# Layer 1's sums of down weights by DMA from DRAM to DRAM during attention, and pairs 2 and 3 of its gate and up by Strassen's scheme

## The chip, the cores and the metric

The kernel runs on one core of a Trainium2 chip. The metric is the device time of one execution in microseconds; the time of a kernel is the median of its runs. Engine names as in the profile: PE is TensorE, PEld its weight loads, DVE is VectorE, ACT is ScalarE, POOL is GpSimd, SP is SyncE, which here only issues DMA.

## The reference

Two decoder layers over x of 512 tokens by 1024 columns. Layer 0 mixes tokens by causal pooling, layer 1 by differential attention with eight heads; behind each mixer stands a gated feed-forward net with 2816 hidden columns, and behind each of the four parts a LayerNorm.

```python
def _swiglu(x, w_gate, w_up, w_down):
    return (jax.nn.silu(x @ w_gate) * (x @ w_up)) @ w_down

def reference(x, pool_w, pool_scale, w_qkv, w_o, lam_p, subln_g, rel_table, w_gate,
              w_up, w_down, ln_mix_g, ln_mix_b, ln_ffn_g, ln_ffn_b):
    for i in range(DEPTH):
        j = i // N_MIXERS
        if i % N_MIXERS == 0:
            h = _multiscale_pool(x, pool_w[j], pool_scale[j])
        else:
            lambda_init = 0.8 - 0.6 * math.exp(-0.3 * i)
            h = _diff_attention(x, w_qkv[j], w_o[j], lam_p[j], subln_g[j], rel_table, lambda_init)
        x = _layernorm(ALPHA * x + h, ln_mix_g[i], ln_mix_b[i])
        x = _layernorm(ALPHA * x + _swiglu(x, w_gate[i], w_up[i], w_down[i]), ln_ffn_g[i], ln_ffn_b[i])
    return x
```

## The kernel before

**Numbers in two halves.** A float32 operand is held as two fp32r tiles: a high half, cast by ScalarE (`h`), and a low half, the operand minus the high half, written by VectorE (`l`). A product is three matmuls: high with high, high with low, low with high (`mm3`, lines 123 to 127, and line 806). All weights lie in one DRAM tensor, `wall`, in pieces of 128 x 1024 in the order of use. SyncE loads them into `raw` (five buffers, line 97), ScalarE and VectorE halve them into weight pairs (six buffers), TensorE multiplies.

**Gate and up.** The function `ffn(layer, late)` (line 449) runs the hidden columns in 11 pairs of 128-column blocks, k and k + 11. A *plain* pair has four chunks of weights, gate and up for both blocks, each against all of x (`plain`, line 758); a chunk is 8 x 3 matmuls of 512 columns. A *Strassen* pair (`strassen`, line 778) has seven products, named P1, Q5, P6, Q3, P7, P2, Q4, each 24 matmuls of 256 columns, into three banks A, C and B. Three products read quarters of x as they are. Four read sums of quarters of x, kept in the tile `xs` as blocks 0 to 3 (for Q5, P6, P7, Q3), each with its high and low half. Four of the seven weights are sums of the pair's four pieces: VectorE adds them in `raw` (line 552) before they are halved. The tuple `SPLIT` (line 47) says which pairs are Strassen pairs: 4 to 10, in both layers.

**The sums of x** are made by the generator `sums_of_x` (line 592), one step at each `next`: four half sums (line 597), four differences and sums of these (lines 612 to 621), with a cast to the high half by ScalarE (line 600) and a low half by VectorE (line 603) for each of the four blocks. The loops call it twice at the start (pair 0) and then twice for every `plain(f)` from f = 3 on (line 765), where f counts blocks, two to a pair.

**The first pairs.** The tokens' last quarters come late, so the first blocks (`early`: three in layer 0, two in layer 1) are run in two halves of the tokens (line 739); f = 2 and 3 are pair 1, f = 4 and 5 pair 2. With each block goes VectorE's product of Silu and up into `hid` (line 584), and with the first four blocks the scale and shift of the last LayerNorm (`affine`, lines 203 and 204, "res" in the profile). After each pair, `sum_hidden` (line 677) makes sums of hidden columns for the down products: four VectorE instructions of 256 columns, a cast, a low half and a store to `ssum`.

**Down.** The product of the hidden columns with the down weights is Strassen's scheme again: P1, Q5, P6, Q3, P7, P2, Q4 over six row groups (`PAIRS`). Four of the seven weight operands are sums of blocks of down weights. They are made during gate and up: for each of 11 rows `load_terms` (line 638) issues three DMAs on GpSimd's queue (two loads, line 651, and one that accumulates, line 652) into free rows of `hid` or the buffer of the LayerNorm parameters; `sum_terms` (line 655) does two VectorE additions of 512 columns (lines 657, 658) and two stores on ScalarE's queue (line 662) to the DRAM tile `tsum`. `weight_sums` (line 671) starts one row, at blocks 0, 1, 3, 5, 7 and at every Strassen pair but the last. The down products load their operands from `wall` and `tsum` (lines 486 and 489).

**Attention.** For every head, TensorE makes values, query and key, transposes the probabilities of the head before, mixes its values and scores the new head. GpSimd has one instruction per head there: the low half of the squares of a head's output (`sql`, line 108, called at 1123), which the sum over squares (`root`, line 1126) of the next head's turn needs.

**What sets the order.** The program runs under a manual schedule: on each engine and each DMA queue, instructions run in the order in which the code emits them; the framework adds only the waits. GpSimd's DMAs stand in GpSimd's own order.

Of the kernel before, what the change touches and what calls it, by code (L numbers as in the profile page):

```python
# [12 lines left out]
F32 = mybir.dt.float32  # L13
# [3 lines left out]
ALU = mybir.AluOpType  # L17

P = 128
# [6 lines left out]
FB = FF // P  # L26
# [17 lines left out]
RAWS = 5  # L44
HALF = FB // 2
DOWN = ("P1", "Q5", "P6", "Q3", "P7", "P2", "Q4")
SPLIT = (4, 5, 6, 7, 8, 9, 10)
GATE = ("P1", "Q5", "P6", "Q3", "P7", "P2", "Q4")
PAIRS = [(0, 2), (2, 2), (4, 2), (6, 2), (8, 2), (10, 1)]

# [2 lines left out]
def trunk(ctx, tc, x, wall, pscale, lam_p, subln, table, lng, lnb, band, first, onehot, out):  # L53
# [386 lines left out]

# [3 lines left out]
    def ffn(layer, late):  # L449
# [5 lines left out]
        with tc.tile_pool(name=f"ffn{layer}", bufs=1) as fp:  # L455
# [6 lines left out]


            order = [k + j * HALF for k in range(HALF) for j in range(2)]
            tsum = dram.tile([4, len(PAIRS), P, 1024], F32, name=f"tsum{layer}")
            ssum = dram.tile([P, 2, 2, HALF, 256], F32, name=f"ssum{layer}")

            def block(i, b):

                if PAIRS[i][1] == 2:  # L470
                    return wall[c1 + 4 * i + b]
                return wall[c1 + 20 + b // 2][:, (b % 2) * 512 : (b % 2 + 1) * 512]


            items = [(p, i) for p in DOWN for i in range(len(PAIRS))]
# [4 lines left out]
            def fetch_item(j):  # L480
                p, i = items[j]
                w = 512 * PAIRS[i][1]
                t = keep.tile([P, 1024], F32, tag="raw", name=f"r{layer}_{j}", bufs=RAWS)[:, :w]
                src = {"P1": 0, "P2": 2, "Q3": 3}
                if p in src:
                    nc.sync.dma_start(out=t, in_=block(i, src[p]))
                else:
                    m = {"Q5": 0, "P6": 3, "P7": 1, "Q4": 2}[p]
                    nc.sync.dma_start(out=t, in_=tsum[m, i, :, :w])
                drops[j] = t  # L490

            def refill():
# [21 lines left out]
            for k in range(HALF):  # L514
                j0 = index[k] = len(chunks)
                c = c0 + 4 * k
                if k in SPLIT:

                    chunks += [(c, ()), (c, (c, c + 1)), (c, (c, c + 2)), (c + 2, ())]
                    chunks += [(c + 1, (c + 1, c + 2)), (c + 3, ()), (c, (c, c + 3))]  # L520
                    step("cast", j0)
                    for w in (
                        "low 0, sum 1, cast 1, sum 4, cast 3, cast 4, low 1, sum 2, cast 2, low 3, "
                        "low 2, sum 6, cast 5, cast 6, low 4, low 5, low 6"
                    ).split(", "):
                        steps.append((w[:-2], j0 + int(w[-1])))
                else:
                    for i in range(4):
                        chunks.append((c + i, ()))
                        step("cast", j0 + i)  # L530
                        step("low", j0 + i)
# [33 lines left out]
            def ahead(upto):  # L565
                advance(upto)
                if upto > len(chunks):
                    prepare(upto - len(chunks), upto - len(chunks))
# [100 lines left out]
            behind = []  # L669

            def weight_sums():
                g = sum_terms(summed_rows[0])
                summed_rows[0] += 1
                next(g)
                behind.append(g)
# [18 lines left out]
            def catch_up():  # L694
                for g in list(behind):
                    if next(g, g) is g:
                        behind.remove(g)
# [35 lines left out]

            early = 3 if layer == 0 else 2
            accs = [(bank(f"g{layer}_{f}"), bank(f"u{layer}_{f}")) for f in range(early)]
            load_terms(0)
            load_terms(1)
            sums = sums_of_x()
            for lo in (0, 256):
                for f in range(early):  # L740
                    for i in range(2):
                        product(accs[f][i], 2 * f + i, lo, lo + 256)
                        if not lo and (f, i) in late:
                            late[f, i]()
                        if not lo:
                            advance(2 * early, True)
                    if lo:
                        advance(2 * f + 6)
                        gated(order[f], *accs[f])
                        affine(n - 1, f)  # L750
                        catch_up()
                        if f < 2:
                            weight_sums()
                            next(sums)
                        if f == 1:
                            behind.append(sum_hidden(0))

            def plain(f):
                k = f // 2
                j = index[k] + 2 * (f % 2)  # L760
                a = (bank(f"g{layer}_{f}"), bank(f"u{layer}_{f}"))
                for i in range(2):
                    product(a[i], j + i, 0, S)
                    ahead(j + i + 5)
                    if f >= 3:
                        next(sums, None)
                    catch_up()
                gated(order[f], *a)
                if f < SB:
                    affine(n - 1, f)  # L770
                if f in (3, 5, 7):
                    weight_sums()
                if f == 3:
                    load_terms(3)
                if f % 2:
                    behind.append(sum_hidden(k))

            def strassen(k):
# [18 lines left out]
                for j, p in enumerate(GATE):  # L797
                    acc = banks[names[p]]
                    h, l = halves[index[k] + j]
                    xh, xl = lefts[p]  # L800
                    for f in range(2):
                        o = acc[:, f * 256 : (f + 1) * 256]
                        for kk in range(4):
                            c = slice((4 * f + kk) * P, (4 * f + kk + 1) * P)
                            for e, (w, x) in enumerate(((h, xh), (h, xl), (l, xh))):
                                nc.tensor.matmul(  # L806
                                    o, w[:, c], x[:, kk, :],
                                    start=p in ("P1", "Q5", "P2") and f + kk + e == 0,
                                    stop=p in ("Q4", "Q3", "P2") and (f, kk, e) == (1, 3, 2),
                                    skip_group_check=True,  # L810
                                )
                    acc = both(acc)
                    if p == "P1":
                        g0 = tile_of(0)
                        nc.scalar.copy(both(g0), acc)
                    elif p == "Q5":
                        nc.scalar.copy(second, acc)
                    elif p == "P6":
                        nc.scalar.copy(first, acc)
                    elif p == "Q3":  # L820
                        tt(first, acc, first, op=ALU.subtract)  # L821
                    elif p == "P7":
                        tt(second, second, acc, op=ALU.subtract)
                    elif p == "P2":
                        tt(both(g0), acc, both(g0), op=ALU.add)  # L825
                    else:
                        g1 = tile_of(1)
                        nc.scalar.activation(both(g1), acc, AF.Silu)
                    ahead(index[k] + j + 6)
                    catch_up()  # L830
                    if p == "P2":
                        nc.scalar.activation(g0, g0, AF.Silu)  # L832
                    elif p == "Q4":
                        tt(first, both(g0), first, op=ALU.mult)
                        tt(second, both(g1), second, op=ALU.mult)
# [3 lines left out]

            f = early  # L840
            while f < FB:
                if f // 2 in SPLIT:
                    strassen(f // 2)
                    f += 2
                else:
                    plain(f)
                    f += 1
# [84 lines left out]
    def attention(late):  # L932
        n = 2
        with tc.tile_pool(name="attn", bufs=1) as ap:
# [225 lines left out]
            for h in range(HEADS):  # L1160
# [19 lines left out]
                if h == 0:  # L1180
                    query(accs[0], w[0], 0, 256)
                    late()
                    query(accs[1], w[1], 0, 256)
                ready(where[0] + 1)
                query(accs[0], w[0], 256 if h == 0 else 0, 512)
                split_query(h, "q", accs[0])
                if h > 0:
# [8 lines left out]
                ready(where[0] + 3)  # L1196
                if h > 0:
                    mix(h - 1)
                start_scores(h)
                score_block(h, 0)  # L1200
                score_block(h, 1)
# [73 lines left out]
def layout(w):  # L1275
# [10 lines left out]
    def ffn(layer):  # L1286
        g = cols(w["w_gate"][layer], P)
        u = cols(w["w_up"][layer], P)
        for k in range(HALF):
            f = [k, k + HALF]  # L1290
            if k in SPLIT:
                halves = [m[f][:, :, h : h + 4] for m, h in ((g, 0), (u, 0), (u, 4), (g, 4))]
                pieces.append(np.stack(halves).transpose(0, 2, 1, 3, 4).reshape(4, P, 1024))
            else:
                pieces.append(np.stack([g[f], u[f]], 1).reshape(4, P, 1024))
# [58 lines left out]
```

## Time and profile before

| | us |
|---|---|
| median of 3 runs (lowest, highest) | 954.47 (954.38, 954.65) |
| the profiled execution, time | 955.13 |
| the profiled execution, span | 953.3 |
| attention, before its output products (395 to 571) | 176 |
| layer 1, gate and up (607 to 837.5) | 230.5 |
| layer 1, down products and the end (837.5 to 953.3) | 115.8 |

The span runs from the first to the last instruction of the profile. Times below are us from its start. A row of a timeline has the start, the duration, the engine, the line of the kernel, the operation, what is written from what, the shape, and in square brackets how long the engine stood idle just ahead and who ended that. Durations of neighbours overlap a little, so the cost of an instruction in a full queue is the distance from its start to the next start.

### The profile page before, as it was taken

Reading aid. Unit: us, or ns where it says so; the run is one execution under the profiler, and the core shown is the slowest. Engines: PE = TensorE matmul, PEld = TensorE weight load, DVE = VectorE, ACT = ScalarE, POOL = GpSimd, SP = SyncE. Lnnn points to the kernel's source line nnn. Section 1 sums busy time; section 2 is a strip of 40 time slices with the busy share of each in tenths; the row PEclk is TensorE's granted clock in tenths of the full one; section 3 lists DMA queues with packets and bytes.
Section 4 is the critical chain, followed back from the end, with each engine's and each line's share of the span. In section 5 each row is a group of like instructions: output and inputs, shape, how many; then the busy total and the mean of one; then the engine's idle time right before and its main releaser. Section 6 shows DMA issues by size and latency. Waiting matters only on the chain.

```text
span 953.3 us, 15380 instructions
## 1 busy us (share of the span) xinstructions
PE 935.9 (98%) x5982; PEld 847.5 (89%) x5982; DVE 779.4 (82%) x1129; ACT 491.4 (52%) x790; POOL 120.6 (13%) x151
## 2 busy tenths in 40 slices
PE   8999999999999999999999999999999999999995
PEld 7898899999988888988888888998899999988884
DVE  6859979999988777688777677789779999987777
ACT  5843335555554457665556553843345554654460
POOL 4311211110001201000000000311111110002102
PEclk9999999999999999999999999999999999999998
DMA  7397988886878964333232222396888785868932
GB/s 207 128 282 241 327 266 266 246 252 205 271 246 269 365 220 134 110 89 100 72 128 79 65 89 89 119 321 203 276 248 256 247 279 199 269 237 291 363 127 89
DMA packets 82248, 197.12 MB, mean 207 GB/s; under 512 B 14804, under 2 KB 26196, under 8 KB 82174
## 3 DMA queue, kind: packets, MB, share of 16 engines
q1 hardware_dynamic: 43052, 115.35, 36.4%
q0 software_dynamic: 15520, 46.14, 17.5%
q10 hardware_dynamic: 23602, 34.63, 10.0%
q8 instruction: 47, 0.77, 0.3%
q14 instruction: 27, 0.22, 0.1%
HBM read 159.38 MB, written 36.72 MB: 206 GB/s over the span
## 4 chain that ended last, share of the span: by engine, by line
PE 92%; DVE 3%; ACT 2%; POOL 1%; DMA 1%; SPq 1%; issue 1%; POOLq 0%; DVEq 0%
PE A L806 17%; PE P L872 13%; PE C L806 8%; PE Q L872 6%; PE B L806 4%; PE u L125 3%; PE u L126 3%; PE u L127 3%; PE g L126 3%; PE g L127 3%; PE g L125 3%; PE s L1062 2%; PE v L125 2%; PE v L126 2%; PE v L127 2%; PE q L126 2%
## 5 line engine op out<-in xcount | busy, mean ns | idle before, releaser
L552 DVE TENSOR_TENSOR raw<-raw,raw 128x1024 f32<-128x1024 f32 x56 | 68.3, 1219 | 0.5
L107 ACT CAST xs<-hid 128x512 fp32r<-128x512 f32 (+1 forms) x60 | 34.7, 582 | 24.3 <-DVE hid L720 24.3
L217 ACT ACTIVATE y<-pt,bT,gT 128x128 f32<-128x128 f32 x96 | 36.1, 456 | 18.1 <-PE pt L212 16.8
L108 DVE TENSOR_TENSOR xs<-hid,xs 128x512 fp32r<-128x512 f32 (+1 forms) x60 | 38.3, 640 | 7.8 <-ACT xs L107 7.8
L1072 ACT ACTIVATE p<-p,mn 128x128 f32<-128x128 f32 (+3 forms) x64 | 35.4, 554 | 14.9 <-DVE mn L1067 14.9
L651 POOL DMA_DIRECT2D b<-in_wall x20 | 14.0, 704 | 172.8 <-DVE g_58l L558 66.7
L712 POOL DMA_DIRECT2D xs<-ssum x24 | 17.4, 725 | 140.3 <-PE Q L872 119.1
L584 DVE TENSOR_TENSOR hid<-sg,u 128x512 f32<-128x512 f32 x16 | 11.0, 685 | 29.4 <-PE u L127 18.7
L108 POOL TENSOR_TENSOR sql<-sq,sqh 128x512 fp32r<-128x512 f32 x7 | 9.1, 1295 | 165.3 <-ACT sqh L107 165.3
L108 DVE TENSOR_TENSOR xt<-y,xt 128x512 fp32r<-128x512 f32 x24 | 16.2, 687 | 16.7 <-ACT xt L107 16.5
L651 POOL DMA_DIRECT2D hid<-in_wall x24 | 18.8, 827 | 82.7 <-DMA tsum<-hid 34.0
L174 POOL TENSOR_SCALAR rs<-mv 128x1 f32<-128x1 f32 x16 | 7.8, 489 | 160.7 <-DVE mv L172 160.7
L1067 DVE CUSTOM_DVE_ANT_0 p<-s,bias 128x128 f32<-128x128 f32 (+3 forms) x64 | 28.0, 484 | 0.0
L688 ACT CAST v<-u 128x512 fp32r<-128x512 f32 x22 | 13.6, 620 | 26.9 <-DVE u L686 26.8
L166 DVE BATCH_NORM_STATS2 st<-res 128x6 f32<-128x512 f32 x32 | 22.2, 694 | 1.1
L832 ACT ACTIVATE sg<-sg 128x512 f32<-128x512 f32 x14 | 8.9, 632 | 25.7 <-DVE sg L825 25.7
L108 DVE TENSOR_TENSOR heads<-k,heads 128x512 fp32r<-128x512 f32 x8 | 5.5, 691 | 20.2 <-ACT heads L107 20.2
L652 POOL DMA_DIRECT2D hid<-in_wall x12 | 14.8, 1232 | 54.0 <-DMA hid<-in_wall 54.0
L600 ACT CAST xs<-hid 128x1024 fp32r<-128x1024 f32 x8 | 8.4, 1051 | 23.8 <-DVE hid L617 11.6
L821 DVE TENSOR_TENSOR hid<-C,hid 128x512 f32<-128x512 f32 x14 | 9.7, 691 | 10.9 <-PE C L806 9.3
L1086 DVE SCALAR_TENSOR_TENSOR p<-p,sm,p 128x128 f32<-128x128 f32 (+3 forms) x32 | 17.6, 551 | 1.1
L107 ACT CAST heads<-k 128x512 fp32r<-128x512 f32 x8 | 4.7, 588 | 26.2 <-PE k L127 26.2
(1118 smaller groups left out, 3746.7 us busy)
## 6 DMA issues: line engine op xcount, KB each, us to landing
raw<-in_wall SPq DMA_DIRECT2D x122, 512.0 KB, 4.6
r<-tsum SPq DMA_DIRECT2D x40, 512.0 KB, 4.0
hid<-in_wall POOLq DMA_DIRECT2D x36, 512.0 KB, 7.0
b<-in_wall POOLq DMA_DIRECT2D x30, 512.0 KB, 5.8
r<-in_wall SPq DMA_DIRECT2D x30, 512.0 KB, 4.4
tsum<-hid ACTq DMA_DIRECT2D x24, 512.0 KB, 5.6
ssum<-v ACTq DMA_DIRECT2D x22, 512.0 KB, 3.9
tsum<-b ACTq DMA_DIRECT2D x20, 512.0 KB, 5.0
```

Of the source, the lines that this page charges most:

```text
L107: nc.scalar.copy(dst_h, src)
L108: (low or nc.vector).tensor_tensor(dst_l, src, dst_h.bitcast(F32), op=ALU.subtract)
L125: nc.tensor.matmul(acc, ah, bh, start=start, stop=False)
L126: nc.tensor.matmul(acc, ah, bl, start=False, stop=False)
L127: nc.tensor.matmul(acc, al, bh, start=False, stop=stop)
L217: nc.scalar.activation(y[:, k, :], pt[:, k * P : (k + 1) * P], AF.Identity, bias=bT[:, n, kk : kk + 1], scale=gT[:, n, kk : kk + 1],)
L552: tt(t, raws[pair[0]], raws[pair[1]], op=ALU.add)
L651: nc.gpsimd.dma_start(out=t[:, j], in_=src[:, j])
L806: nc.tensor.matmul(o, w[:, c], x[:, kk, :], start=p in ("P1", "Q5", "P2") and f + kk + e == 0, stop=p in ("Q4", "Q3", "P2") and (f, kk, e) ...
L872: nc.tensor.matmul(accs[s], x[:, k, r], y[:, c], start=first and k == 0 and e == 0, stop=last and k == m - 1 and e == 2, skip_group_check= ...
L1067: nc.vector.tensor_tensor_reduce(out=p, in0=accs[c][:, :w], in1=biases[h][:, w - 1 :: -1] if w < S else biases[h][:, ::-1], op0=ALU.add, o ...
L1072: nc.scalar.activation(p, p, AF.Exp, bias=mn[:, q, c : c + 1], scale=-1.0, accum_out=sm[:, q, c : c + 1],)
```

## The change

There are two changes to layer 1; layer 0 keeps its own.

The sums of its down weights are no longer made in its gate and up. Twenty-four DRAM tiles `sums` (four sums, six row groups) are filled by a generator `sum_steps`, whose transfers all go from DRAM to DRAM on GpSimd's queue: a copy of one block, then an accumulating transfer of a second block; two of the four sums start from a copy of another sum. A step issues three transfers, and attention takes two steps per head, 48 transfers in 16 steps. In layer 1 `load_terms` and `weight_sums` do nothing more, so 33 loads on GpSimd's queue, 22 additions on VectorE and 22 stores on ScalarE's queue go.

Pairs 2 and 3 of layer 1 become Strassen pairs, with their weights laid out for it. For this the sums of x are made one block earlier: two steps of the generator for each `plain(f)` from f = 2 on, and what is left after the products of the first Strassen pair.

```diff
-SPLIT = (4, 5, 6, 7, 8, 9, 10)
+SPLIT = ((4, 5, 6, 7, 8, 9, 10), (2, 3, 4, 5, 6, 7, 8, 9, 10))
...
+    sums = [
+        [dram.tile([P, 512 * m], F32, name=f"t1_{q}_{i}") for i, (_, m) in enumerate(PAIRS)]
+        for q in range(4)
+    ]
+
+    def block(c, i, b):
+
+        if PAIRS[i][1] == 2:
+            return wall[c + 4 * i + b]
+        return wall[c + 20 + b // 2][:, (b % 2) * 512 : (b % 2 + 1) * 512]
+
+    def sum_steps(c):
+
+        for q, start, b in ((0, None, 1), (1, None, 3), (3, 0, 3), (2, 3, 2)):
+            for adds in range(2):
+                for i in range(len(PAIRS)):
+                    if adds:
+                        source, op = block(c, i, b), dict(accum_op=ALU.add)
+                    else:
+                        source, op = sums[start][i] if start is not None else block(c, i, q), {}
+                    nc.gpsimd.dma_start(
+                        out=sums[q][i], in_=source, max_dma_last_dim=8192, **op
+                    )
+                    if i % 3 == 2:
+                        yield
+
+    terms_of_1 = sum_steps(total - FB)
...
-                    nc.sync.dma_start(out=t, in_=tsum[m, i, :, :w])
+                    nc.sync.dma_start(out=t, in_=sums[m][i] if layer else tsum[m, i, :, :w])
...
-                if k in SPLIT:
+                if k in SPLIT[layer]:
...
             def weight_sums():
+                if layer:
+                    return
...
-            load_terms(0)
-            load_terms(1)
-            sums = sums_of_x()
+            if not layer:
+                load_terms(0)
+                load_terms(1)
+            xsums = sums_of_x()
...
-                    if f >= 3:
-                        next(sums, None)
+                    if f >= 3 - layer:
+                        next(xsums, None)
...
-                if f == 3:
+                if f == 3 and not layer:
                     load_terms(3)
...
                     ahead(index[k] + j + 6)
+                    next(xsums, None)
                     catch_up()
...
                 ready(where[0] + 1)
+                next(terms_of_1, None)
                 query(accs[0], w[0], 256 if h == 0 else 0, 512)
...
                     mix(h - 1)
+                next(terms_of_1, None)
                 start_scores(h)
```

Two places in the order of the engines show what moved.

VectorE, before, in layer 1 while TensorE is at pair 2. The rows run from the low half of chunk g_13 (pair 3) to the hid row of block 5: `L603` rows write the low halves of `xs` (blocks 2, 1 and 3 in that order; block 0 stands ahead of these rows), `L621` is the last sum of x, and both stand among the low halves of pair 3's weights.

```order
L558 TENSOR_TENSOR g_13l<-raw_6684,g_13h 128x1024
L621 TENSOR_TENSOR hid_6342<-hid_6342 128x1024
L603 TENSOR_TENSOR xs_6343<-hid_6342,xs_6343 128x1024
L584 TENSOR_TENSOR hid_6342<-sg_2_6857,u_4_6778 128x512
L558 TENSOR_TENSOR g_14l<-raw_6722,g_14h 128x1024
L603 TENSOR_TENSOR xs_6343<-hid_6342,xs_6343 128x1024
L690 TENSOR_TENSOR v_1_6818<-u_1_6817,v_1_6818 128x2x256
L558 TENSOR_TENSOR g_15l<-raw_6755,g_15h 128x1024
L603 TENSOR_TENSOR xs_6343<-hid_6342,xs_6343 128x1024
L584 TENSOR_TENSOR hid_6342<-sg_13_6926,u_5_6861 128x512
```

The same sums of x now. The rows run from the third difference (`L642`, block 1) to the low half of block 1; the three `L628` rows are the low halves of blocks 0, 2 and 1. `L609` is the hid row of block 3, the last of pair 1, `L577` a weight sum of pair 2, and g_12 and g_13 are pair 2's fifth and sixth products.

```order
L642 TENSOR_TENSOR hid_6414<-hid_6414 128x1024
L628 TENSOR_TENSOR xs_6415<-hid_6414,xs_6415 128x1024
L717 TENSOR_TENSOR v_0_6708<-u_0_6707,v_0_6708 128x2x256
L646 TENSOR_TENSOR hid_6414<-hid_6414 128x1024
L628 TENSOR_TENSOR xs_6415<-hid_6414,xs_6415 128x1024
L609 TENSOR_TENSOR hid_6414<-sg_12_6825,u_3_6760 128x512
L203 TENSOR_TENSOR res<-res,gb_5297 128x1024
L204 TENSOR_TENSOR res<-res,gb_5297 128x1024
L577 TENSOR_TENSOR raw_6589<-raw_6589,raw_6664 128x1024
L583 TENSOR_TENSOR g_12l<-raw_6598,g_12h 128x1024
L583 TENSOR_TENSOR g_13l<-raw_6664,g_13h 128x1024
L628 TENSOR_TENSOR xs_6415<-hid_6414,xs_6415 128x1024
```

The low half of block 1 stood behind the hid row of pair 2's first block and more than a pair ahead of its first reader, pair 4's third product; now it stands behind the hid row of pair 1's last block and the weights of pair 2's fifth and sixth product, and its reader is pair 2's third product.

GpSimd, before, in attention: the low halves of the squares follow one another, one per head.

```order
L108 TENSOR_TENSOR sql_4868<-sq_4866,sqh_4867 128x512
L108 TENSOR_TENSOR sql_5115<-sq_5113,sqh_5114 128x512
L108 TENSOR_TENSOR sql_5351<-sq_5349,sqh_5350 128x512
L108 TENSOR_TENSOR sql_5596<-sq_5594,sqh_5595 128x512
L108 TENSOR_TENSOR sql_5827<-sq_5825,sqh_5826 128x512
```

GpSimd now, between two of them (`t_q_i` is row group i of sum q).

```order
L108 TENSOR_TENSOR sql_4913<-sq_4911,sqh_4912 128x512
L463 DMA t_1_3_540<-in_wall 64x2048
L463 DMA t_1_4_541<-in_wall 64x2048
L463 DMA t_1_5_542<-in_wall 128x512
L463 DMA t_3_0_549<-t_0_0_531 64x2048
L463 DMA t_3_1_550<-t_0_1_532 64x2048
L463 DMA t_3_2_551<-t_0_2_533 64x2048
L108 TENSOR_TENSOR sql_5166<-sq_5164,sqh_5165 128x512
```

Six transfers stand between two of them, here three that accumulate into sum 1 and three copies of sum 0 into sum 3.

More of the change, by code (lines that the diff above doesn't have):

```diff
@@ L464, in ffn @@
             order = [k + j * HALF for k in range(HALF) for j in range(2)]
-            tsum = dram.tile([4, len(PAIRS), P, 1024], F32, name=f"tsum{layer}")
+            if not layer:
+                tsum = dram.tile([4, len(PAIRS), P, 1024], F32, name="tsum")
             ssum = dram.tile([P, 2, 2, HALF, 256], F32, name=f"ssum{layer}")
[L468 to L472, printed above, removed]
             items = [(p, i) for p in DOWN for i in range(len(PAIRS))]
@@ L485, in fetch_item @@
                 if p in src:
-                    nc.sync.dma_start(out=t, in_=block(i, src[p]))
+                    nc.sync.dma_start(out=t, in_=block(c1, i, src[p]))
                 else:
                     m = {"Q5": 0, "P6": 3, "P7": 1, "Q4": 2}[p]
-                    nc.sync.dma_start(out=t, in_=tsum[m, i, :, :w])
+                    nc.sync.dma_start(out=t, in_=sums[m][i] if layer else tsum[m, i, :, :w])
                 drops[j] = t
@@ L735, in ffn @@
             accs = [(bank(f"g{layer}_{f}"), bank(f"u{layer}_{f}")) for f in range(early)]
-            load_terms(0)
-            load_terms(1)
-            sums = sums_of_x()
+            if not layer:
+                load_terms(0)
+                load_terms(1)
+            xsums = sums_of_x()
             for lo in (0, 256):
@@ L753, in ffn @@
                             weight_sums()
-                            next(sums)
+                            next(xsums)
                         if f == 1:
@@ L841, in ffn @@
             while f < FB:
-                if f // 2 in SPLIT:
+                if f // 2 in SPLIT[layer]:
                     strassen(f // 2)
@@ L1290, in ffn @@
             f = [k, k + HALF]
-            if k in SPLIT:
+            if k in SPLIT[layer]:
                 halves = [m[f][:, :, h : h + 4] for m, h in ((g, 0), (u, 0), (u, 4), (g, 4))]
```

## The prediction

> **What bounds the kernel now.** I read three views in this order: the page's busy times, the busy times by stage, and the timeline of single engines where the change works (layer 1's gate and up, from 607 us on). A stage's row gives its stretch and length, then the busy us (and instructions) of TensorE, its weight loads, VectorE, ScalarE and GpSimd, the granted clock, the DMA share and GB/s.
>
> ```profile
> PE 935.9 (98%) x5982; PEld 847.5 (89%) x5982; DVE 779.4 (82%) x1129; ACT 491.4 (52%) x790; POOL 120.6 (13%) x151
> 395.00:571.00 176.00, 176.00 (x1115) 153.98 (x1114) 135.89 (x317) 104.11 (x234) 9.06 (x7) 1.00 0.29 90
> 632.00:696.40 64.40, 64.40 (x287) 53.33 (x286) 52.46 (x61) 20.16 (x25) 10.74 (x12) 1.00 0.82 254
> 654.00:676.00 22.00, 22.00 (x99) 18.22 (x98) 19.71 (x23) 8.46 (x11) 4.98 (x6) 1.00 0.79 259
> 696.40:716.60 20.20, 20.20 (x171) 20.20 (x170) 18.34 (x22) 9.22 (x11) 2.69 (x3) 1.00 0.82 260
> ```
>
> TensorE never rests in these stages: attention (395 to 571), the plain pairs (to 696) and the Strassen pairs after them. VectorE is second and close: 19.71 of 22.00 us in the plain pairs, 18.34 of 20.20 in a Strassen pair. So the change can win only what it takes off TensorE, and it loses wherever it makes TensorE wait for VectorE.
>
> **What TensorE gains.** The rows are the first matmuls of chunks g_8, g_12 and g_16, the start of the first Strassen product of pair 4 and the start of the down products, behind pair 10.
>
> ```profile
> 652.76 0.39 PE L125 MATMUL g<-xt,g_8h 128*128 128x512 f32 x1
> 674.52 0.39 PE L125 MATMUL g<-xt,g_12h 128*128 128x512 f32 x1
> 696.28 0.40 PE L806 MATMUL A<-xt,g_16h 128*128 128x256 f32 x2
> ...
> 696.44 2.87 PE A L806 x24
> 837.55 14.99 PE P L872 x66
> ```
>
> A plain pair takes 674.52 - 652.76 = 21.76 us, and so does the next. Seven Strassen pairs take 837.55 - 696.44 = 141.11 us, 20.16 each, 2.88 per product. Two pairs exchanged: 2 x 1.60 = **-3.2 us**. That is all there is to win.
>
> **What VectorE must do first.** Pair 2 now begins its Strassen products where g_8 began, at 652.8. With nothing to wait for, Q5 follows at 655.6, P6 at 658.5, Q3 at 661.4. They read the sums of x in xs: block 0 for Q5, 1 for P6, 3 for Q3, each with a low half that VectorE writes in its turn. Before, nobody read xs until after 699. How long the turn takes I add up from the starts of VectorE's instructions before.
>
> ```profile
> 625.48 0.69 DVE L584 TENSOR_TENSOR hid<-sg,u 128x512 f32<-128x512 f32 x1 [4.46 <-PE u L127]
> 626.09 1.22 DVE L203 TENSOR_TENSOR res<-res,gb 128x1024 f32<-128x1024 f32 x1
> 627.34 1.23 DVE L204 TENSOR_TENSOR res<-res,gb 128x1024 f32<-128x1024 f32 x1
> 628.48 0.68 DVE L657 TENSOR_TENSOR hid<-hid 128x512 f32<-128x512 f32 x1
> ...
> 629.81 1.22 DVE L597 TENSOR_TENSOR hid<-xt 128x1024 f32<-128x1024 f32 x1
> 630.95 1.21 DVE L558 TENSOR_TENSOR g_6l<-raw,g_6h 128x1024 fp32r<-128x1024 f32 x1
> ...
> 639.81 0.42 DVE L683 TENSOR_TENSOR u<-hid 128x256 f32<-128x256 f32 x1
> ...
> 641.40 1.22 DVE L558 TENSOR_TENSOR g_9l<-raw,g_9h 128x1024 fp32r<-128x1024 f32 x1
> ...
> 649.08 0.68 DVE L690 TENSOR_TENSOR v<-u,v 128x512 fp32r<-128x512 f32 x1
> 649.68 1.22 DVE L558 TENSOR_TENSOR g_11l<-raw,g_11h 128x1024 fp32r<-128x1024 f32 x1
> 650.81 1.22 DVE L612 TENSOR_TENSOR hid<-hid 128x1024 f32<-128x1024 f32 x1
> 652.06 1.23 DVE L614 TENSOR_TENSOR hid<-hid 128x1024 f32<-128x1024 f32 x1
> ...
> 654.90 0.69 DVE L584 TENSOR_TENSOR hid<-sg,u 128x512 f32<-128x512 f32 x1 [1.61 <-ACT sg L583]
> ...
> 670.44 1.22 DVE L603 TENSOR_TENSOR xs<-hid,xs 128x1024 fp32r<-128x1024 f32 x1
> ```
>
> Starts lie 0.61 us apart after a 512-wide instruction (0.60 for v), 1.14 after a 1024-wide one, 1.25 where the next reads its result; the four of a hidden sum take 1.59. The queue of the changed kernel is the same up to 625.48, when the second layer's first hid row is written (that waits for TensorE, which is unchanged so far). From there to the low half of xs block 1 it holds 3 hid rows before pair 2 and one inside it (4 x 0.61 = 2.4), 4 affine pairs (4 x 2.39 = 9.6), 4 half sums of x and 4 differences of them (4.6 + 4.8), 8 low halves of weights (g_6 to g_13, 9.1), the 4 sums of pair 2's weights (4.6), one hidden sum with its low half (2.2) and 3 low halves of xs (3.4): 40.7 us. Of the 15 us of down-weight sums that go (22 instructions of 0.68), only three pairs stood ahead of this point, 4 us, and pair 2's own weight sums take that back.
>
> ScalarE adds waits. The hid row of f = 2 needs its Silu, which now stands behind two casts of xs and one of v:
>
> ```profile
> 641.52 0.63 ACT L688 CAST v<-u 128x512 fp32r<-128x512 f32 x1 [2.33 <-DVE u L686]
> ...
> 653.32 1.05 ACT L600 CAST xs<-hid 128x1024 fp32r<-128x1024 f32 x1 [0.21 <-DVE hid L614]
> ...
> 654.28 0.59 ACT L583 ACTIVATE sg<-g 128x512 f32<-128x512 f32 x1
> ```
>
> Step by step: 625.48 plus hid, affine, half sum, two low halves is 631.9; hid, affine, half sum, g_8l, two half sums, hidden sum give 641.05; weight sums 1 and 4, g_9l, two differences end at 647.05; the casts then run to 648.1 and, with v, the Silu to 649.15, a wait of 2.1 us (1.61 at this place before). Affine, sum 2, g_11l, g_10l and a difference follow, and **xs 0 is complete at 658.05**. Then v, a difference, xs 2, and a second wait, 0.5 us, for the Silu of f = 3; hid at 661.4, affine, sum 6, g_12l, g_13l, and **xs 1 is complete at 669.0**; the next hidden sum, g_14l, then **xs 3 at 672.9**.
>
> TensorE therefore stands 658.05 - 655.65 = 2.4 us in Q5, which then ends at 660.9; 669.0 - 660.9 = 8.1 us in P6; 672.9 - 671.9 = 1.0 in Q3: **+11.5 us**. Nothing covers it: behind the waiting matmul stand all later products on TensorE. VectorE is free of it afterwards: carried on by the same steps, g_17l is there at 684.6 and needed at 690.6, g_22l at 693.7 and needed at 704.9. Its sums of down weights are gone from every later pair, so I expect no stall there, and no gain either, since TensorE sets 20.16. ScalarE's three more casts for each of the two pairs hide in its idle half (9.22 of 20.20 busy in a Strassen pair).
>
> **Bounds of this term.** Without the Silu waits, xs 1 comes after 40.7 us at 666.2; the stalls are then 0.3, 7.4 and 1.0, 8.7 together. The other way, if each wait for another engine grows by 1 us, some 13.5. I take 11.5, the sum with the waits by their rows.
>
> **The clock after the stall.** This happened once near the start.
>
> ```profile
> 27.89 1.07 PE L212 MATMUL pt<-ident,res 128*128 128x128 f32 x8 [1.39 <-DVE res L184]
> 30.16 0.42 PE L127 MATMUL mix<-pw0h,pooled 128*128 128x256 f32 x1
> 30.38 0.41 PE L125 MATMUL mix<-pw0h,pooled 128*128 128x256 f32 x1
> ...
> 29.50:30.00 0.50, 0.50 (x5) 0.44 (x3) 0.47 (x2) 0.50 (x2) 0.50 (x1) 0.52 0.00 0
> 32.50:33.00 0.50, 0.50 (x4) 0.50 (x4) 0.50 (x2) 0.27 (x1) 0.00 (x0) 0.56 0.81 328
> ```
>
> After 1.39 us of idleness and light work the granted clock was about 0.5 from 29.5 to 32.7, and matmuls came 0.22 us apart instead of 0.12 (2.88 / 24): 15 of them, 1.4 us lost. After 8.1 us of idleness P6 should restart slow. 1.4 us lost there eats Q3's 1.0 us of waiting: **+0.4 us**. Twice that stretch gives +1.8, no slow clock 0. The Trainium skill, TensorE: Matmul & The Clock Gate, What's actually happening, says the gate falls to half after an idle window of about 3.4 us and opens only after a busy one; the rows agree. By that rule an estimate for this stall is 0.4 to 2 us, since the window does not start with the work.
>
> **The DMA in attention.** 48 transfers on GpSimd's queue, 40 of 512 KB and 8 of 256 KB: 22.5 MB in about 176 us, 128 GB/s on top of the 90 above, 218, below the 254 that the plain pairs move without a stall. Six stand between two of GpSimd's sql instructions.
>
> ```profile
> 442.82 1.29 POOL L108 TENSOR_TENSOR sql<-sq,sqh 128x512 fp32r<-128x512 f32 x1 [21.30 <-ACT sqh L107]
> 449.99 0.70 ACT L1132 ACTIVATE rso<-ss,eps_t 128x512 f32<-128x512 f32 x1
> ...
> 610.11 1.52 POOL L651 DMA_DIRECT2D hid<-in_wall  x2
> 615.58 1.25 POOL L652 DMA_DIRECT2D hid<-in_wall  x1 [3.96 <-DMA hid<-in_wall]
> ...
> hid<-in_wall POOLq DMA_DIRECT2D x36, 512.0 KB, 7.0
> ```
>
> A head has 22.5 us of which GpSimd idled 21.3. Two loads issued at 610.1 had landed by 615.6: 2.7 us each, six in 16.4 us. Issue takes GpSimd 6 x 0.76 to 1.25 us. I take **0**: idle GpSimd and DMA cover it, and a late sql has 449.99 - 444.11 = 5.9 us until its sum is read. No row shows a copy from DRAM to DRAM. From below the cost is 0, for nothing is taken out of attention; from above, 7.0 us each one after another make 42 us a head (the rival below). I stay near the pair of 610.1, which shows two in flight. The loads and stores that leave layer 1's gate and up were no one's bound, since TensorE never waited there: also 0.
>
> **Sum.** -3.2 + 11.5 + 0.4 = +8.7. The profiled run took 955.13 (span 953.3 and 1.8 around it), so 963.8 by its own time; it lies 0.7 over the median of 954.47, so I forecast **963.2**.
>
> **Rivals.** *TensorE stays the bound (faster).* If xs 1 were complete by 658.6, only the -3.2 would be left: 951.3. The point is VectorE's queue from 625.48: it would have to take 33 us, not 43. For it speaks that VectorE idled 4.46 us just ahead; against it, its order is fixed, and before, with nearly as much ahead of it, the low half of xs 1 started at 670.44. Chance 0.08. Between the two lie stalls of half my size, 0.05 for a result within 0.2%, about what a measurement of this kernel can tell from no change.
>
> *Attention waits for the sums.* If six transfers take longer than 22.5 us, GpSimd's waits hold up sql, and TensorE waits for it in each of seven heads. Reading and writing DRAM at twice 16.4 gives 32.8: (32.8 - 22.5) x 7 - 5.9 = +66 us, 1029; at 24 us a head +5, 968. Against it: in the order a row waits on what was issued at least six transfers earlier, and the DMA share is 0.29. Chance 0.13. The Trainium skill, DMA: Bandwidth & Descriptors, Issuing engines are not separate DMA queues, says that all queues share the 16 engines, so the raw loads of attention compete with this; no run here shows that yet.
>
> *VectorE as I say, size off*: inside the forecast's own range, 959.5 to 967, chance 0.74.
>
> **Range.** Eight in ten: 957.5 to 974, the forecast's range, half of the smaller stalls and the cheap half of the second rival. Faster by over 0.2%: 0.07; within: 0.05; slower: 0.88.
>
> **What would show it.** Right: in the profile after, TensorE idle ahead of the C and A products of pair 2, released by VectorE's xs, 7 to 9 us at one place; a stretch of clock near 0.5 behind it; pair 4 starting some 8 to 9 us later than 696.3; attention's length unchanged; 20.16 us per pair. Wrong: pair 2 without idle time; idle TensorE in attention ahead of the sums over squares; or pairs 3 to 10 longer than 20.2.

## The result and the profile after

| | us |
|---|---|
| median of 6 runs after (lowest, highest) | 963.68 (961.88, 966.97) |
| median of 6 runs before, on the same chip | 954.46 (953.56, 956.17) |
| ratio after to before, 95% interval | 1.009 [1.0075, 1.0105] |
| the profiled execution after, time and span | 961.88, 959.9 |

The changed kernel is 0.9% slower, 9.2 us by the medians. Busy times first, from the page after: the engine, its busy us, share of the span, instructions; then TensorE's busy tenths in 40 slices of 24 us and the granted clock in the same slices.

```profile
PE 934.7 (97%) x6126; PEld 853.3 (89%) x6126; DVE 784.6 (82%) x1127; ACT 499.8 (52%) x802; POOL 122.6 (13%) x166
PE   8999999999999999999999999996999999999995
PEclk9999999999999999999999999997999999999998
```

TensorE's busy time barely changed (935.9 before), yet the span grew: one slice, 648 to 672 us, has a 6 for busy and a 7 for the clock. That is pair 2. The timeline of TensorE there, after:

```profile
650.97 0.40 PE L834 MATMUL A<-xt,g_8h 128*128 128x256 f32 x2
...
656.31 0.39 PE L834 MATMUL C<-xs,g_9h 128*128 128x256 f32 x1 [2.19 <-DVE xs L628]
...
660.38 0.41 PE L834 MATMUL A<-xs,g_10h 128*128 128x256 f32 x1
667.28 0.58 PE L834 MATMUL A<-xs,g_10h 128*128 128x256 f32 x1 [6.49 <-DVE xs L628]
```

The row at 650.97 starts P1, the one at 656.31 belongs to Q5, into C, the last two to P6, into A. Q5 and P6 each run its first matmul, high half with high half, and then stand until VectorE has written the low half of their block of `xs`. The timeline of VectorE, after, has these writes (`L628`) and what the queue before them waited for:

```profile
623.70 0.69 DVE L609 TENSOR_TENSOR hid<-sg,u 128x512 f32<-128x512 f32 x1 [4.46 <-PE u L127]
...
647.37 0.69 DVE L609 TENSOR_TENSOR hid<-sg,u 128x512 f32<-128x512 f32 x1 [2.13 <-ACT sg L608]
...
655.04 1.22 DVE L628 TENSOR_TENSOR xs<-hid,xs 128x1024 fp32r<-128x1024 f32 x1
...
659.60 0.69 DVE L609 TENSOR_TENSOR hid<-sg,u 128x512 f32<-128x512 f32 x1 [0.47 <-ACT sg L608]
...
666.01 1.22 DVE L628 TENSOR_TENSOR xs<-hid,xs 128x1024 fp32r<-128x1024 f32 x1
...
669.87 1.22 DVE L628 TENSOR_TENSOR xs<-hid,xs 128x1024 fp32r<-128x1024 f32 x1
```

From the first hid row to the second of these writes VectorE is idle for 2.6 us of 42: this is a full queue, and TensorE waits for its end. The chain of waits, after, shows what follows (start, length, engine, target, line, matmuls; a piece of 5.76 is the last product of one pair and the first of the next, both into A):

```profile
667.28 4.75 PE A L834 x23
672.03 2.88 PE C L834 x24
...
680.67 5.76 PE A L834 x48
...
700.83 5.76 PE A L834 x48
...
844.83 14.99 PE P L901 x66
```

From 680.67 to 700.83 is 20.16: from pair 3 on all Strassen pairs run at TensorE's own pace. The chain dates a product 0.16 to 0.17 us behind the start of its first matmul, so the length of the pairs is taken from the timeline. The first matmul of pair 4, after:

```profile
703.54 0.40 PE L834 MATMUL A<-xt,g_22h 128*128 128x256 f32 x2
```

Pair 2 starts at 650.97, so pairs 2 and 3 took 52.57 us; before, as plain pairs, they took 696.28 - 652.76 = 43.52. That is 9.05 us more.

The first hid row stands at 625.48 before and 623.70 after. In the eight experiments it lies anywhere from 623.83 to 626.47, with the DMA sums and without, so this is no gain of the change. By these 1.78 us, and by an end that is 0.67 us shorter (not shown to come from the change either), the two profiled spans are only 6.6 us apart. The distance from that row to the first down product is free of both; each row of the table is one execution:

| kernel | Strassen pairs of layer 1 | first hid row to down products | against before |
|---|---|---|---|
| before | 4 to 10 | 625.48 to 837.39 | |
| after | 2 to 10 | 623.70 to 844.66 | +9.05 |
| E1, DMA sums alone | 4 to 10 | 624.90 to 836.81 | 0.00 |
| E2, DMA sums, pair 3 | 3 to 10 | 624.60 to 834.91 | -1.60 |
| E3, LayerNorm's scale and shift late | 2 to 10 | 626.47 to 838.85 | +0.47 |
| E4, sums of x early | 2 to 10 | 624.85 to 839.26 | +2.50 |
| E5, both | 2 to 10 | 624.11 to 832.81 | -3.21 |
| E6, the old sums kept | 2 to 10 | 623.83 to 850.88 | +15.14 |
| E8, four more VectorE additions | 2 to 10 | 623.83 to 849.12 | +13.38 |
| E9, more DMA traffic in attention | 3 to 10 | 625.86 to 836.17 | -1.60 |

### The profile page after: what moved, and what is told of

Read it like the earlier page. It is cut to its first block, busy times and chain, and to the rows that moved or that the text cites. A ratio compares the mean times of both kernels' runs of the same rounds, so it can differ in the third digit from the quotient of the medians.

```text
span 959.9 us, 15639 instructions
## 1 busy us (share of the span) xinstructions
PE 934.7 (97%) x6126; PEld 853.3 (89%) x6126; DVE 784.6 (82%) x1127; ACT 499.8 (52%) x802; POOL 122.6 (13%) x166
## 4 chain that ended last, share of the span: by engine, by line
PE 88%; DVE 7%; ACT 2%; issue 1%; POOL 1%; POOLq 0%; DVEq 0%; ACTq 0%
PE A L834 19%; PE P L901 13%; PE C L834 9%; PE Q L901 6%; PE B L834 5%; PE g L126 2%; PE u L127 2%; PE u L125 2%; PE u L126 2%; PE g L127 2%; PE g L125 2%; PE s L1091 2%; PE v L125 2%; PE v L127 2%; PE v L126 2%; PE q L126 2%
## 5 line engine op out<-in xcount | busy, mean ns | idle before, releaser
L577 DVE TENSOR_TENSOR raw<-raw,raw 128x1024 f32<-128x1024 f32 x64 | 78.0, 1219 | 0.5
L463 POOL DMA_DIRECT2D t<-in_wall x36 | 25.8, 944 | 5.3 <-DMA t<-in_wall 5.3
L609 DVE TENSOR_TENSOR hid<-sg,u 128x512 f32<-128x512 f32 x12 | 8.2, 686 | 22.2 <-PE u L127 15.9
L715 ACT CAST v<-u 128x512 fp32r<-128x512 f32 x22 | 13.7, 621 | 22.8 <-DVE u L713 22.7
L861 ACT ACTIVATE sg<-sg 128x512 f32<-128x512 f32 x16 | 10.1, 633 | 29.5 <-DVE sg L853 29.5
L845 ACT COPY hid<-C 128x512 f32<-128x512 f32 x16 | 9.4, 587 | 20.8 <-PE C L834 20.8
L1091 PE MATMUL s<-heads 64*128 64x256 f32 (+2 forms) x192 | 17.9, 330 | 0.0
L676 POOL DMA_DIRECT2D b<-in_wall x10 | 7.0, 703 | 85.0 <-DVE g_58l L583 34.2
```

Source lines behind the costliest of these rows:

```text
L577: tt(t, raws[pair[0]], raws[pair[1]], op=ALU.add)
L1091: nc.tensor.matmul(accs[c][:, :wide], a[r, qs], b[r, :wide], start=i == 0, stop=i == 2)
```

## The experiments

The experiments bear the numbers E1 to E6, E8 and E9; there is no E7. The theory: the loss is VectorE's queue between the second layer's first hid row and the `xs` halves of pair 2, and nothing else; the DMA sums cost nothing and each Strassen pair is worth 1.60 us. Rivals: the DMA sums slow attention or the down products; or the Strassen pairs lose by themselves, by more work on ScalarE or VectorE. Each result below is the median of the runs against that of the kernel before in the same series of runs; the ratio stands with its 95% interval, and is not exactly the quotient of the two medians.

**E1 and E2: the parts of the change.** E1 keeps the DMA sums, and the sums of x one block earlier, and goes back to Strassen pairs 4 to 10. E2 adds pair 3 alone.

```diff
-SPLIT = ((4, 5, 6, 7, 8, 9, 10), (2, 3, 4, 5, 6, 7, 8, 9, 10))
+SPLIT = ((4, 5, 6, 7, 8, 9, 10), (4, 5, 6, 7, 8, 9, 10))          # E1
+SPLIT = ((4, 5, 6, 7, 8, 9, 10), (3, 4, 5, 6, 7, 8, 9, 10))       # E2
```

> Only the first half of the change: layer 1's sums of down weights by DMA during attention, pairs 2 and 3 plain as before. VectorE's queue theory (TensorE waits in pair 2 for the sums of x): no stall, TensorE's work as before, 954.5 (953.2 to 955.8); the 15 us taken from VectorE are worth nothing. Rival 1, the transfers in attention cost time: 957 or more, up to the full 963.7.

> As the change, but pair 2 stays plain and only pair 3 becomes a Strassen pair; the sums of x then have one plain pair, 21.8 us, more before they are read. VectorE's queue theory: no stall in pair 3, 1.6 us less TensorE work than before: 952.9 (951.6 to 954.2). Rival 2, each added Strassen pair costs more than it saves (half of the loss each): about 959. Rival 1: 961 or more.

E1: 954.23 against 954.6, ratio 0.9998 [0.9985, 1.0011]. E2: 952.11 against the same 954.6, ratio 0.9975 [0.9961, 0.9988]. Neither has a wait of TensorE in gate and up. So the DMA sums alone make no difference that can be measured (E1's interval leaves 0.15% at most), though they take 22 additions off VectorE and 22 stores off ScalarE's queue: those engines were not the bound there. And one Strassen pair, where it does not wait, gains 1.60 us in the table. The loss needs pair 2.

**E3: shorten the queue.** The scale and shift of the last LayerNorm for layer 1, four pairs of additions and multiplications, move from the first four blocks to the pairs from 3 on.

```diff
-                        affine(n - 1, f)
+                        if not layer:
+                            affine(n - 1, f)
...
-                if f < SB:
+                if f < SB and not layer:
                     affine(n - 1, f)
...
+                if layer and k >= 3:
+                    z, gb = res[:, (k - 3) // 2, :], gbs[n - 1]
+                    tt(z, z, gb[:, (k - 3) % 2, :], op=ALU.add if (k - 3) % 2 else ALU.mult)
```

> As the change, but in layer 1 the scale and shift of the last LayerNorm (four pairs of VectorE instructions, 9.6 us) no longer stand ahead of pair 2: one instruction goes behind each of pairs 3 to 10. VectorE's queue theory, by the running sum: xs 0 in time, xs 1 about 2.5 us late, xs 3 about 1 us late: -3.2 + 3.5 against before, 954.8 (953 to 957). Rival 2: the same work later, no change against the change, 963.7. Rival 1: 961 or more.

955.0 against 954.6, ratio 1.0005 [0.9991, 1.0019]. The timelines of TensorE and of VectorE, E3:

```profile
662.22 0.39 PE L835 MATMUL A<-xs,g_10h 128*128 128x256 f32 x1 [2.44 <-DVE xs L628]
666.08 0.38 PE L835 MATMUL C<-xs,g_11h 128*128 128x256 f32 x1 [0.73 <-DVE xs L628]
```

```profile
626.47 0.69 DVE L609 TENSOR_TENSOR hid<-sg,u 128x512 f32<-128x512 f32 x1 [4.46 <-PE u L127]
...
660.95 1.22 DVE L628 TENSOR_TENSOR xs<-hid,xs 128x1024 fp32r<-128x1024 f32 x1
```

The low half of block 1 now comes 34.5 us after the first hid row instead of 42.3, and TensorE's idle time falls from 8.7 to 3.2 us. What the two pairs gain, 3.2 us, is lost again in the waits: no difference can be measured.

**E4: start the sums of x earlier.** Three steps of the generator go ahead of the second half of the tokens.

```diff
             for lo in (0, 256):
+                if lo and layer:
+                    for _ in range(3):
+                        next(xsums)
                 for f in range(early):
```

> As the change, but in layer 1 the first three steps of the sums of x (four half sums, 4.6 us) are issued before the second half of the tokens, where VectorE stood idle for 4.46 us, so every later step comes earlier in the queue and all low halves of xs stand ahead of pair 2's first reader; the LayerNorm's scale and shift stay where they are. VectorE's queue theory, by the running sum: xs 1 at 648, xs 3 at 656, no stall, 951.3 (950 to 952.8), faster than both kernels. Rival 2 (VectorE has too much work, whatever its order): 960 or more. Rival 1: 961 or more.

956.75 against 954.6, ratio 1.0022 [1.0009, 1.0035]: a miss by 5.5 us. VectorE wrote block 1 at 647.64 and block 3 at 655.93, in good time, but TensorE waited all the same. Its timeline, E4:

```profile
659.53 0.50 PE L837 MATMUL A<-xs,g_10h 128*128 128x256 f32 x2 [1.49 <-ACT sg L846]
664.87 0.51 PE L837 MATMUL C<-xs,g_11h 128*128 128x256 f32 x2 [2.20 <-ACT hid L848]
```

The releaser is now ScalarE, and its timeline says why (`L846` and `L848` copy the results of P1 and Q5 out of banks A and C, which P6 and Q3 then fill):

```profile
657.84 0.52 ACTq L719 DMA_DIRECT2D ssum<-v  x1
658.41 0.60 ACT L608 ACTIVATE sg<-g 128x512 f32<-128x512 f32 x1 [3.65 <-PE C L837]
658.90 0.58 ACT L846 COPY sg<-A 128x512 f32<-128x512 f32 x1
...
663.29 1.04 ACT L580 CAST g_14h<-raw 128x1024 fp32r<-128x1024 f32 x1 [2.86 <-DVE raw L577]
664.24 0.58 ACT L848 COPY hid<-C 128x512 f32<-128x512 f32 x1
```

On VectorE, E4:

```profile
657.07 0.68 DVE L717 TENSOR_TENSOR v<-u,v 128x512 fp32r<-128x512 f32 x1
...
660.89 1.23 DVE L204 TENSOR_TENSOR res<-res,gb 128x1024 f32<-128x1024 f32 x1
662.03 1.22 DVE L577 TENSOR_TENSOR raw<-raw,raw 128x1024 f32<-128x1024 f32 x1
```

The two copies stand in ScalarE's order behind things that hang on VectorE. The copy of P1 is behind the store of `ssum`, which needs the low half of v at 657.07; the cast of g_14, a sum of weights (`raw`, `L577`) made at 662.03 behind LayerNorm's scale and shift, stands ahead of the copy of Q5. The Silu's row names PE C as its releaser, but what ended last ahead of it on ScalarE is the store. In the changed kernel the two copies start at 659.47 and 664.81, as late as here; there the longer wait for `xs` covers them. So VectorE's queue is the cause here too, one step removed, and the expectation had not followed it through ScalarE.

The waits are not the whole of it. From start to start they are 1.65 and 2.36 us, 4.0 together, and with the gain of 3.2 that would leave +0.8; the table has +2.50. Behind the second wait TensorE's clock is about half for a while. The busy times, E4 (us, busy us and instructions of TensorE, its weight loads, VectorE, ScalarE, GpSimd, clock, DMA share, GB/s):

```profile
666.00:669.50 3.50, 3.50 (x19) 3.50 (x19) 3.47 (x6) 1.11 (x2) 0.00 (x0) 0.52 0.74 286
```

Q3 takes 669.15 - 664.87 = 4.28 us instead of 2.88, and its two neighbours lose another 0.3: that is the remaining 1.7.

**E5: E3 and E4 together.** If that reading holds, shortening VectorE's queue in both ways leaves no wait.

> Both edits together: the half sums of x in VectorE's idle time before the second half of the tokens, and layer 1's scale and shift behind pairs 3 to 10. In the run with the early sums alone TensorE no longer waited for xs but 3.7 us for two ScalarE copies, which stood behind casts and a Silu that waited for VectorE instructions behind scale and shift. Theory (queue order on VectorE and, behind it, ScalarE): with 9.6 us less ahead of these, no stall in pair 2, -3.2 against before: 951.3 (950 to 952.8). If the added Strassen pairs cost TensorE or ScalarE something of their own: 953 to 956.

951.2 against 954.16, ratio 0.9971 [0.9956, 0.9986]. The chain of waits, E5, from pair 2 on:

```profile
651.54 2.87 PE A L838 x24
654.42 2.88 PE C L838 x24
...
668.82 5.76 PE A L838 x48
...
688.98 5.76 PE A L838 x48
```

The products follow each other every 2.88 us and both pairs take 20.16. From the first hid row to the down products E5 is 3.21 us shorter than before, twice the 1.60 of the sum. This version is faster than both kernels; from E2, whose interval is nearly the same, the runs do not tell it apart.

**E6: the old sums kept.** Pairs 2 and 3 by Strassen's scheme on the kernel before, with the sums of x one block earlier as in the change, but with the sums of down weights still made by VectorE. The half sums of x and the loaded blocks of down weights share rows of `hid` here, so part of layer 1's sums of down weights are not the right ones; the amount of work is.

```diff
-SPLIT = (4, 5, 6, 7, 8, 9, 10)
+SPLIT = ((4, 5, 6, 7, 8, 9, 10), (2, 3, 4, 5, 6, 7, 8, 9, 10))
...
-                    if f >= 3:
+                    if f >= 3 - layer:
                         next(sums, None)
...
                     ahead(index[k] + j + 6)
+                    next(sums, None)
                     catch_up()
```

> Only the second half of the change: pairs 2 and 3 by Strassen's scheme with the sums of x one block earlier, and layer 1's sums of down weights made in gate and up as before. Theory: VectorE has three pairs of sums, 4 us, more ahead of xs 1, and the half sums must also wait for the stores of the first sums, which leave the same rows: stalls 4 to 8 us longer than the change's, 968 to 972. If the sums of down weights did not stand in the way: 963.7.

969.3 against 954.16, ratio 1.0157 [1.0132, 1.0182]. The timelines of TensorE and VectorE, E6:

```profile
660.37 0.58 PE L806 MATMUL C<-xs,g_9h 128*128 128x256 f32 x1 [6.11 <-DVE xs L603]
672.66 0.58 PE L806 MATMUL A<-xs,g_10h 128*128 128x256 f32 x1 [7.18 <-DVE xs L603]
```

```profile
623.83 0.69 DVE L584 TENSOR_TENSOR hid<-sg,u 128x512 f32<-128x512 f32 x1 [4.46 <-PE u L127]
...
646.82 1.23 DVE L612 TENSOR_TENSOR hid<-hid 128x1024 f32<-128x1024 f32 x1 [1.18 <-DMA tsum<-hid]
...
671.39 1.22 DVE L603 TENSOR_TENSOR xs<-hid,xs 128x1024 fp32r<-128x1024 f32 x1
```

Block 1 is 47.56 us behind the first hid row, 5.25 later than in the changed kernel: the sums of down weights and 1.18 us of waiting for their stores, which comes from the shared rows. So the DMA sums are not idle in the change. They are worth 6.1 us by the table (15.14 - 9.05): 5.25 in this queue, the rest in more matmuls at the slow clock behind the waits (P6's 23 matmuls take 5.08 us here, 4.59 in the changed kernel). To a kernel with pairs 4 to 10 they are worth nothing (E1).

**E8: a longer queue.** Four 1024-wide additions more (the half sums for blocks 0 and 2 written three times) in the queue ahead of `xs`.

```diff
-                whole(r0, 1, 0)
-                whole(r1, 1, 1)
+                for _ in range(3 if layer else 1):
+                    whole(r0, 1, 0)
+                    whole(r1, 1, 1)
```

> The change with four half sums of x of 1024 columns repeated (same result) on VectorE in layer 1, ahead of xs 0 and xs 1. Theory, one to one: 4 x 1.14 = 4.6 us longer than the change, 968.2 (967 to 969.5). If VectorE's queue is not what TensorE waits for: 963.7.

967.05 against 954.16, ratio 1.0128 [1.0106, 1.0149]. On VectorE's timeline, E8, the low half of block 1:

```profile
670.68 1.22 DVE L628 TENSOR_TENSOR xs<-hid,xs 128x1024 fp32r<-128x1024 f32 x1
```

It starts 46.85 us behind the first hid row, 4.54 later than after: 4 x 1.14 = 4.56. The table has 4.33 of them arrive at the down products; the medians, 967.05 and 963.68, from two series of runs, are 3.4 apart, and 967.05 is only just inside the expected range. What VectorE does there comes out at the end nearly one for one.

**E9: more DMA in attention.** E2 with one more copy from DRAM to DRAM beside every copy of the sums, into tiles that nobody reads: 24 transfers more, 72 in all.

```diff
+                    if not adds:
+                        nc.gpsimd.dma_start(
+                            out=extra[q][i], in_=block(c, i, q), max_dma_last_dim=8192
+                        )
```

> The version with pair 3 alone by Strassen's scheme (952.1, no stall in gate and up), with 24 further copies of 512 or 256 KB from DRAM to DRAM in attention into tiles that nobody reads: 72 transfers, 34 MB. If attention has room for the transfers: 952.1 as without them. If they are near what it can hide: TensorE waits in attention for raw weights or for sql, 955 or more.

952.66 against 954.16, ratio 0.9984 [0.9971, 0.9997], with E2 at 0.9975 [0.9961, 0.9988]: no difference that these intervals show. The table of distances begins behind attention, so it cannot show one. Attention itself, with its output products, is as long with the transfers as without:

| kernel | attention's first query matmul | first gate matmul of layer 1 | distance |
|---|---|---|---|
| before | 383.65 | 606.99 | 223.34 |
| after | 381.88 | 605.21 | 223.33 |
| E1, DMA sums alone | 383.07 | 606.40 | 223.33 |
| E9, 72 transfers | 384.00 | 607.36 | 223.36 |

The busy times of attention, after and then E9 (columns as in E4):

```profile
395.00:571.00 176.00, 176.00 (x1108) 153.63 (x1107) 137.58 (x319) 104.17 (x234) 34.85 (x46) 1.00 0.76 205
```

```profile
395.00:571.00 176.00, 176.00 (x1116) 154.08 (x1115) 136.03 (x316) 103.73 (x234) 46.85 (x67) 1.00 0.94 273
```

What GpSimd waits for there, E9 (us in total, times, longest):

```profile
POOL sql L108 <- ACT sqh L107: 103.4, 7, 19.8
```

GpSimd still waits 103.4 / 7 = 14.8 us for each `sql`, so it is never late, and TensorE never rests. The transfers themselves do slow each other. Median time to landing in attention, before, after and in E9:

```profile
raw<-in_wall SPq DMA_DIRECT2D x24, 512.0 KB, 3.5
```

```profile
raw<-in_wall SPq DMA_DIRECT2D x24, 512.0 KB, 4.8
t<-in_wall POOLq DMA_DIRECT2D x22, 512.0 KB, 8.8
```

```profile
t<-in_wall POOLq DMA_DIRECT2D x25, 512.0 KB, 13.1
raw<-in_wall SPq DMA_DIRECT2D x24, 512.0 KB, 8.8
```

Attention's weights take 3.5, 4.8 and 8.8 us, and are asked for early enough for all three.

## Why the prediction was right, and where it was off

**TensorE's gain, -3.2: right.** E5 shows it alone, -3.21; E2 shows half of it.

**VectorE's queue, +11.5: right in cause and size.** From the first hid row to the low half of block 1 the sum had 42.38 us (complete at 669.0, less 1.14 for the instruction itself and 625.48); the trace has 42.31. The two waits for the Silu were forecast at 2.1 and 0.5 and came at 2.13 and 0.47. Q5's stall was forecast at 2.4 and is listed as 2.19 (2.3 from start to start, since a listed wait begins at the modelled end of the matmul before). P6's, forecast at 8.1, is listed as 6.49 because Q5 ended 1.3 us late on a slow clock; from the point where Q5 would have ended at full clock it is 8.1. Q3's 1.0 does not show, because P6 ran slow for longer than that. E3, E6 and E8 move block 1 by -7.8, +5.25 and +4.54 us, and the time follows.

**The clock, +0.4: mis-sized.** Behind the waits Q5's matmuls took 660.38 - 656.31 = 4.07 us and P6's, to the start of Q3 at 671.87, 4.59; 23 matmuls at 0.12 are 2.76. Q5's loss of 1.3 went under in P6's wait; of P6's 1.8, 1.0 took the place of Q3's wait and 0.8 is left. I had put P6's loss at the 1.4 us of the one slow stretch near the start, and had not expected that a wait as short as Q5's slows the clock too. I had also read an idle window into the rows near the start: from 26.1 to 29.5, just ahead of that slow stretch, TensorE has 2.01 us of work. The term is +0.8 instead of +0.4, inside its bounds of 0 to 1.8. With it the sum is -3.2 + 11.5 + 0.8 = 9.1, and the trace has 9.05. That the forecast of 963.2 and the median of 963.68 agree to 0.5 us is closer than the runs can tell: the interval is 1.4 us to either side.

**The DMA in attention, 0: right.** E1 and the length of attention show it, and E9 shows that there is room for half as many transfers again. The rival in which attention waits for the sums is out: six transfers a head never reached `sql`. I had 218 GB/s for attention (48 transfers of these sizes are 23.1 MB and not 22.5, which makes it 221); it is 205. The Trainium skill, DMA: Bandwidth & Descriptors, Issuing engines are not separate DMA queues, has all queues share the 16 engines; the landing times of `raw`, 3.5, 4.8 and 8.8 us, agree with that, and here it cost nothing. The down products, which now load their sums from the 24 tiles, take no longer either: 959.9 - 844.83 = 115.1 us to the end, 115.8 before.

**The rival in which TensorE stays the bound** is out for the change itself, but E5 is that case, made by two moves of code: its 951.2 is the rival's 951.3.

**The signs.** TensorE waited for `xs` ahead of the C and A products of pair 2, a clock of about 0.5 followed, attention kept its length, and a pair took 20.16 us from pair 3 on. Two sizes lay outside what I had named: the longest wait is 6.49 us and not 7 to 9, for the reason above, and pair 4 starts 7.26 us later than before by the profile's times, or 9.04 counted from the first hid row.

**What was not in the forecast** is E4: I had followed VectorE's queue only as far as `xs`. ScalarE's copies of P1 and Q5 hang on the same queue a little later, and a forecast for a kernel with `xs` on time would have missed them, as the expectation of E4 did.

Not tried: E5's moves with the old sums. Its early sums of x need rows of `hid` that the old sums hold at that time.

## What to carry to other kernels

A step that makes the bounding engine faster also moves its reads forward, and a full in-order queue on another engine does not move with them. Add up that queue, from an instruction whose time is fixed to the write that the moved read needs, with start-to-start distances and the waits in it, and compare with the new deadline: here the sum held to 0.1 us. Before calling a cure for one wait complete, do the same for every other thing the next product needs, the emptying of its bank too.

## What the hardware showed

**The clock goes by stretches of fixed length, not by the length of a wait.** The busy times after, in stretches of 3.4 us from 654.0 (columns as above):

```profile
654.00:657.40 3.40, 1.21 (x11) 1.09 (x10) 3.40 (x4) 1.04 (x1) 0.00 (x0) 1.00 0.42 145
657.40:660.80 3.40, 3.39 (x18) 3.10 (x16) 2.93 (x4) 2.77 (x4) 0.00 (x0) 0.53 0.44 154
660.80:664.20 3.40, 0.00 (x0) 0.00 (x0) 3.37 (x4) 0.53 (x2) 0.00 (x0) 0.97 0.00 0
664.20:667.60 3.40, 0.32 (x1) 0.32 (x2) 3.37 (x4) 2.13 (x3) 0.00 (x0) 0.53 0.35 100
667.60:671.10 3.50, 3.50 (x18) 3.50 (x18) 3.47 (x6) 0.62 (x1) 0.00 (x0) 0.50 0.53 212
671.10:674.50 3.40, 3.40 (x29) 3.40 (x29) 1.73 (x2) 0.59 (x1) 0.00 (x0) 0.98 0.43 145
```

The stretches begin close to where the clock changes, and these changes lie 3.4 us or twice that apart. Each row's clock goes with TensorE's busy time in the row above it: after 1.21 us of work it is about half, after 3.39 full, though TensorE then does nothing, after 0.00 and 0.32 half, after 3.50 full. The Trainium skill, TensorE: Matmul & The Clock Gate, What's actually happening, states a free-running window of 3413 ns; the trace agrees, with 13.7 us from 657.4 to 671.1 as four of them. The page's table has the gate fall after an idle window; here one with 1.21 us of work sufficed, and before, near the start, one with 2.01 (26.1 to 29.5). In E4 one with 2.24 us (655.8 to 659.2) left the clock at full.

So the wait of 2.19 us in Q5 was followed by half a clock, though its first matmuls still ran at full, and in E3 one of 2.44 us left the clock at full all the way. The busy times, E3, from just ahead of the wait's end:

```profile
662.00:665.40 3.40, 3.13 (x24) 2.93 (x24) 3.33 (x7) 0.75 (x2) 0.00 (x0) 1.00 0.66 264
```

The stretches of E3 from 652 to 672 have 1.00 too. That E3's wait was divided between two windows is argued from this, not shown.

**Copies and accumulating transfers from DRAM to DRAM** of 512 KB landed in 9 to 14 us (medians after and in E9), several in flight, and 72 of them beside attention's own loads brought the DMA share to 0.94. Only GpSimd waited for a transfer there, and its own slack took it.
